# An mLSTM scan's element-wise steps: scalings and decay exponentials on ScalarE, the mask behind them, two directions joined from PSUM, and silu formed without GpSimd

## The chip, the cores and the metric

The kernel runs on one core of a Trainium2 chip. Its time is the device time of one execution in microseconds (us). Five engines work side by side, each through its own row of instructions, strictly in order: TensorE (PE, matrix products into PSUM banks), VectorE (DVE), ScalarE (ACT), GpSimd (POOL) and SyncE (SP, which issues most DMAs). A profile counts PE's loading of weights as a line of its own (PEld).

## The reference, cut to what matters

The program is one step of a two-layer network over 1024 sample tokens and 128 prompt tokens, 1024 features wide. The first layer has four bidirectional mLSTM heads and grouped-query attention side by side, the second has neighbourhood attention. Each branch is multiplied by silu(z) of the same input projection.

```python
def step(carry, xs):                      # one 128-token chunk of one mLSTM head, one direction
    C, n, m = carry
    b = jnp.cumsum(lf, axis=-1)
    Dm = jnp.where(causal, b[..., :, None] - b[..., None, :] + li[..., None, :], -jnp.inf)
    ...
    P = jnp.exp(Dm - m_t[..., None]) * jnp.einsum('bhld,bhsd->bhls', qj, kj)
    num = w_inter[..., None] * jnp.einsum('bhvk,bhlk->bhlv', C, qj) + jnp.einsum('bhls,bhsv->bhlv', P, vj)
    den = ...
    h = num / jnp.maximum(jnp.abs(den), jnp.exp(-m_t))[..., None]
    ...
    wk = jnp.exp(g - m_new[..., None])
    C_new = a_st[..., None, None] * C + jnp.einsum('bhs,bhsv,bhsk->bhvk', wk, vj, kj)
...
ha = rmsnorm(h_f + rev(h_b), g_hn) * jax.nn.sigmoid(oa)
...
y = jnp.concatenate([ha, from_heads(hb)], axis=-1) * jax.nn.silu(z)
```

## The kernel before

The 1152 tokens are nine chunks of 128, taken three at a time as groups of 384 columns (`CW`). The program goes through phases: the norms and modulations (`front`), the gates and the projections of heads 0 and 1, the mLSTM scan of heads 0 to 3, grouped-query attention, its output, neighbourhood attention in eight pairs of heads, and the last output. Most of PE's work are projections in 32-bit split into a high and a low part: three products per block (L371, L372, L373) into one of two PSUM banks called `pj`. `weights` makes the high part of a weight tile on ACT (L114) and the low one on POOL (L115, 128x1024).

The order of the work around the change is not written by hand. A scheduler builds each engine's row from the program and its own model of durations, so that an edit in one step can move its neighbours. Only in the attention phases does PE's row follow the program text. In the scan, the projections of the next heads, the second layer's modulation rows (L252, a custom DVE operation on 128x512) and the scan's own steps are mixed by it.

One head of the scan (`mlstm`) runs as follows.
- Seven times, `update` scales the keys of one chunk per direction into `kw` (L670, two buffers), multiplies them with the values into a bank called `o` (L673), and DVE adds the product to the decayed state `cs` (L680). Head by head this is a chain of eight.
- Then three groups. `decays` takes the tile `e`, which `decays_load` fetched by DMA (L644, issued in ACT's row while the head before was in the same group, three buffers), and turns it into decays: subtract (L653, POOL), mask (L656, POOL), exponential (L658, ACT). DVE multiplies by the scores (L711). Matmuls fill one PSUM bank per direction, `po` (L717 and L719, banks named `s`).
- `den` is formed from the banks; DVE scales both directions (L732) and adds them (L733) into `hs`. ACT squares `hs` (L736), POOL forms the reciprocal root (L133, L134), POOL scales `hs` (L739), and PE transposes it (L106, bank `tr`). DVE multiplies by the gate tile `gt` (L750).

The gate tile comes from projections: `oev` (tanh L609 on ACT, scaling L610 on POOL, by `ghn`) and `zev`, which calls `silu_gate` (tanh L395 on ACT, L396 on POOL, product L397 on DVE). `silu_gate` also serves the gates `gz` of both attentions: 48 calls, 12 of them in the mLSTM heads.

Of the kernel before, what the change touches and what calls it, by code (L numbers as in the profile page):

```python
# [12 lines left out]
AF = mybir.ActivationFunctionType  # L13
ALU = mybir.AluOpType
# [4 lines left out]
P = 128  # L19
# [9 lines left out]
NEG = -1e30  # L29
# [10 lines left out]
class Kern:  # L40
# [350 lines left out]
    def silu_gate(self, out, ps):  # L391

        nc = self.nc
        th = self.st([P, CW], n="th")
        nc.scalar.activation(th, ps, AF.Tanh, scale=0.5)  # L395
        nc.gpsimd.tensor_scalar(th, th, 0.5, 0.5, ALU.mult, ALU.add)  # L396
        nc.vector.tensor_tensor(out, th, ps, ALU.mult)  # L397


    def gates_proj(self, h):  # L400
# [165 lines left out]
    def mlstm_proj(self, hd):  # L566

        nc = self.nc
        new = lambda n: self.u(([P, NT, P + (n == "v")] if n in "kv" else [P, T]), n=n)
        o = {}  # L570

        def tok3(src, dst):
            for g in range(NC):
                pt = self.ps("ptr")
                for i in range(3):
                    s = (3 * g + i) * P
                    self.flipped(pt[:, i * P : (i + 1) * P], src[:, s : s + P])
                self.evac(dst[:, 3 * g : 3 * g + 3, 0:P], pt[:, :CW].rearrange("p (a b) -> p a b", b=P))

        def qev(c, ps):  # L580
            if c == 0:
                o["q"] = new("qT")
            for y, x in self.rows(o["q"], c, ps):
                self.evac(y, x)

        def kev(c, ps):
            if c == 0:
                o["kT"] = new("kT")
            for y, x in self.rows(o["kT"], c, ps):
                nc.scalar.activation(y, x, AF.Copy, scale=float(P) ** -0.5)  # L590
            if c == 2:
                o["k"] = new("k")
                tok3(o["kT"], o["k"])

        def vev(c, ps):
            if c == 0:
                o["vT"] = new("vT")
            for y, x in self.rows(o["vT"], c, ps):
                self.evac(y, x)
            if c == 2:  # L600
                v = o["v"] = new("v")
                nc.vector.memset(v[:, :, P], 1.0)
                tok3(o["vT"], v)

        def oev(c, ps):
            if c == 0:
                o["g"] = new("gate")
            g = o["g"][:, c * CW : (c + 1) * CW]
            nc.scalar.activation(g, ps, AF.Tanh, scale=0.5)  # L609
            nc.gpsimd.tensor_scalar(g, g, 1.0, self.ghn[:, hd : hd + 1], ALU.add, ALU.mult)  # L610

        def zev(c, ps):
            z = self.st([P, CW], n="z")
            self.silu_gate(z, ps)
            g = o["g"][:, c * CW : (c + 1) * CW]
            nc.vector.tensor_tensor(g, g, z, ALU.mult)

        return lambda: [o[n] for n in ("q", "kT", "k", "v", "g")], (qev, kev, vev, oev, zev)
# [28 lines left out]
    def decays(self, hd, g, t):  # L647

        nc = self.nc
        e, wb = t[:, 0:2], t[:, 2:4]  # L650
        ev = e.rearrange("p d (c l) -> p d c l", l=P)
        av = self.nat[:, 0, 3 * g : 3 * g + 3, :].rearrange("p c (d h) -> p h d c", d=2)[:, hd]
        nc.gpsimd.tensor_tensor(ev, av[:, :, :, None].to_broadcast([P, 2, 3, P]), ev, ALU.subtract)  # L653
        for d in range(2):
            s = 1 if d == 0 else -1
            nc.gpsimd.affine_select(out=ev[:, d], in_=ev[:, d], pattern=[[0, 3], [s, P]], compare_op=ALU.is_ge, fill=NEG, base=0, channel_multiplier=-s)  # L656
        ef = e.rearrange("p d l -> p (d l)")
        nc.scalar.activation(ef, ef, AF.Exp)  # L658
        return e, wb

    def mlstm(self, hd, cs, order, qT, kT, k, v, gt):
        nc, a = self.nc, self.a
        nat = self.nat
        P1 = P + 1

        def update(chs):

            kw = self.t("kw", 2, [P, 2, P])
            for d in range(2):
                nc.gpsimd.tensor_tensor(kw[:, d, :], k[:, chs[d], :], nat[:, 1, chs[d], 4 * d + hd : 4 * d + hd + 1].to_broadcast([P, P]), ALU.mult)  # L670
            pu = self.ps("o")
            for d in range(2):
                nc.tensor.matmul(pu[:, d * P1 : (d + 1) * P1], kw[:, d, :], v[:, chs[d], :], start=True, stop=True)  # L673
            return [pu[:, d * P1 : (d + 1) * P1] for d in range(2)]
# [28 lines left out]
        for g in range(NC):  # L703
            e, wb = self.decays(hd, g, ts[g])
            ql = qT[:, g * CW : (g + 1) * CW]
            nc.vector.tensor_tensor(wb, wb, ql[:, None, :].to_broadcast([P, 2, CW]), ALU.mult)
            pst = self.ps("s")
            for i in range(3):
                s = (3 * g + i) * P
                nc.tensor.matmul(pst[:, i * P : (i + 1) * P], kT[:, s : s + P], qT[:, s : s + P], start=True, stop=True)  # L710
            nc.vector.tensor_tensor(e, e, pst[:, None, :CW].to_broadcast([P, 2, CW]), ALU.mult)  # L711
            po = [self.ps("s") for _ in range(2)]
            for i in range(3):
                ch = 3 * g + i
                for d in range(2):
                    o = po[d][:, i * P1 : (i + 1) * P1]
                    nc.tensor.matmul(o, e[:, d, i * P : (i + 1) * P], v[:, ch, :], start=True, stop=ch == 8)  # L717
                    if ch < 8:
                        nc.tensor.matmul(o, wb[:, d, i * P : (i + 1) * P], cs[d][:, ch, :], start=False, stop=True)  # L719
            den = self.sm(6)  # L720
            hs = self.t("hs", 2, [P, 3, P])
            hb = self.t("hb", 1, [P, 3, P])
            for d in range(2):
                pv = po[d][:, : 3 * P1].rearrange("p (c l) -> p c l", l=P1)
                nc.scalar.activation(den[:, 3 * d : 3 * d + 3], pv[:, :, P], AF.Abs)
            floor = nat[:, 2, 3 * g : 3 * g + 3, :].rearrange("p c (d h) -> p d c h", d=2)[:, :, :, hd]
            dv = den[:, :6].rearrange("p (d c) -> p d c", d=2)
            nc.vector.tensor_tensor(dv, dv, floor, ALU.max)
            nc.vector.reciprocal(den[:, :6], den[:, :6])
            for d in range(2):  # L730
                pv = po[d][:, : 3 * P1].rearrange("p (c l) -> p c l", l=P1)
                nc.vector.tensor_tensor((hs, hb)[d], pv[:, :, 0:P], den[:, 3 * d : 3 * d + 3, None].to_broadcast([P, 3, P]), ALU.mult)  # L732
            nc.vector.tensor_tensor(hs, hs, hb, ALU.add)  # L733
            ss = self.sm(3)
            for i in range(3):
                nc.scalar.activation(hb[:, i, :], hs[:, i, :], AF.Square, accum_out=ss[:, i : i + 1])  # L736
            rs = self.sm(3)
            self.rstd(rs[:, :3], ss[:, :3], P)
            nc.gpsimd.tensor_tensor(hs, hs, rs[:, :3, None].to_broadcast([P, 3, P]), ALU.mult)  # L739
            if hd + 1 < HA:  # L740
                self.ts.append(self.decays_load(hd + 1, g))
            pt = self.ps("tr")
            for i in range(3):
                self.flipped(pt[:, i * P : (i + 1) * P], hs[:, i, :])
            for i in range(3):
                ch = 3 * g + i
                src = pt[:, i * P : (i + 1) * P]
                if ch < 8:
                    src = self.by_rows(src)
                nc.vector.tensor_tensor(self.cols(y, ch), src, self.cols(gt, ch), ALU.mult)  # L750
# [153 lines left out]
    def gqa_scores(self, Q, kv, new, prs):  # L904

        nc = self.nc
        zero = self.zero[:, 0:1].to_broadcast([P, CW])
        for hh in range(2):
# [11 lines left out]
            r = self.smg(1)  # L920
            nc.scalar.activation(pr, pr, AF.Exp, bias=nm, scale=-1.0, accum_out=r)
            nc.vector.reciprocal(r, r)
            for c in range(NC):
                nc.gpsimd.tensor_scalar(pr[:, c, :], pr[:, c, :], r, 1.0, ALU.mult, ALU.mult)  # L924
            prs.append(pr)
            yield

# [94 lines left out]
    def ctx_steps(self, S, V, tmp, po=None, banks=("tr", "s")):  # L1022
# [9 lines left out]
        r = self.sm(2)  # L1032
        for hh in range(2):
            nc.scalar.activation(pr[:, hh, :], s[hh], AF.Exp, bias=nm[:, hh : hh + 1], accum_out=r[:, hh : hh + 1])
        nc.vector.reciprocal(r[:, :2], r[:, :2])
        nc.gpsimd.tensor_tensor(pr, pr, r[:, :2, None].to_broadcast([P, 2, P]), ALU.mult)
        yield
# [212 lines left out]
    def na_unit(self, terms, v, vc, bias, j, po):  # L1250
# [15 lines left out]
        for hh in range(2):  # L1266
# [5 lines left out]
            r = self.sm(1)  # L1272
            nc.scalar.activation(x, x, AF.Exp, bias=nm, scale=-1.0, accum_out=r)  # L1273
            nc.vector.reciprocal(r, r)  # L1274
            nc.gpsimd.tensor_scalar(x, x, r, 1.0, ALU.mult, ALU.mult)  # L1275
            tr = self.ps(("tr", "ptr")[hh])
            for i in range(nk):
                self.flipped(tr[:, i * P : (i + 1) * P], x[:, i * P : (i + 1) * P])
# [14 lines left out]
    def run(self):  # L1293
# [11 lines left out]
        with self.phase("front"):  # L1305
# [2 lines left out]
            self.mod0 = self.const([P, KB, 2, 2], "mod0")  # L1308
            self.shift[0], self.scale[0] = self.mod0[:, :, 0], self.mod0[:, :, 1]
            self.ghn = self.const([P, 4], "ghn")  # L1310
            nc.vector.tensor_scalar(self.ghn, self.par[:, 80:84], 0.5, None, ALU.mult)
            h = [self.chunk("h") for _ in range(NC)]


# [323 lines left out]
```

## Time and profile before

| | |
|---|---|
| median of 3 runs | 1554.34 us (1553.78 to 1555.73) |
| the profiled execution | 1554.8 us, of which its span 1553.0 |
| granted TensorE clock, mean | 0.995 |
| busy in the span: PE, DVE, ACT, POOL | 1499.3, 846.4, 653.0, 609.9 us |
| chain of work that ended last | PE 83%, DVE 6%, DMA 3%, POOL 2%, ACT 2%, issue 2% |
| instructions | 27156 |

A line of the profile such as L653 is a line of the kernel file; a group is written output<-inputs with partitions x elements. Time under an engine is time in which it worked; the idle time before an instruction is put down to what released it last. An engine that is idle costs nothing unless the chain that ends last runs through it.

### The profile page before, as it was taken

The page shows a single profiled execution, that of the slowest core. Times are in us where ns is not written, and L with a number is a line of the kernel's source. Part 1 is how long each engine was busy: PE and PEld are TensorE (multiplying, and loading weights), DVE is VectorE, ACT ScalarE, POOL GpSimd, SP SyncE. Part 2 cuts the span into 40 slices and gives each one's busy share as a digit, 9 for nine tenths or more (in the row PEclk, how much of TensorE's full clock was granted, in tenths as well). Part 3 has the DMA queues.
Part 4 walks back from the last instruction along what each step waited for, and adds up shares of the span by engine and source line. Part 5 has one row for each costly group of instructions (what it writes and reads, how often), then busy time and mean ns, then how long its engine had stood idle before and what let it go on. Part 6 is the DMA issues. An engine that isn't in the chain of part 4 may idle for free.

```text
span 1553.0 us, 27156 instructions
## 1 busy us (share of the span) xinstructions
PE 1499.3 (97%) x10164; PEld 1380.9 (89%) x10164; DVE 846.4 (55%) x2342; ACT 653.0 (42%) x1573; POOL 609.9 (39%) x830
## 2 busy tenths in 40 slices
PE   7899999999999899999999999999999999999998
PEld 5799998999999888777788989999999999989886
DVE  5732997974547856665465452435243434345532
ACT  4622212112235767778344452445243434345411
POOL 3414645644445835577133332333142314243200
PEclk9999999999999999999999999999999999999999
DMA  9212634431220000021334212131213121225342
GB/s 354 81 42 102 219 124 182 158 113 65 104 93 32 17 23 32 24 72 49 134 108 159 74 52 87 34 105 27 90 44 97 31 84 39 87 76 151 128 130 82
DMA packets 75011, 143.80 MB, mean 93 GB/s; under 512 B 15928, under 2 KB 46848, under 8 KB 74880
## 3 DMA queue, kind: packets, MB, share of 16 engines
q1 hardware_dynamic: 70294, 126.91, 24.7%
q10 hardware_dynamic: 4586, 15.16, 2.6%
q8 instruction: 80, 1.31, 0.3%
q14 instruction: 51, 0.42, 0.1%
HBM read 115.47 MB, written 21.86 MB: 88 GB/s over the span
## 4 chain that ended last, share of the span: by engine, by line
PE 83%; DVE 6%; DMA 3%; POOL 2%; ACT 2%; issue 2%; SPq 0%; DVEq 0%; POOLq 0%; ACTq 0%
PE pj L371 12%; PE pj L373 12%; PE pj L372 12%; PE pj L386 7%; PE pj L387 7%; PE pj L388 7%; PE s L914 4%; PE ptr L106 4%; PE o L954 4%; PE o L1288 4%; PE s L1265 3%; PE tr L106 3%; DVE mj L252 2%; PE pj L106 2%; DMA wm<-in_w_mod_dram 1%
## 5 line engine op out<-in xcount | busy, mean ns | idle before, releaser
L371 PE MATMUL pj<-hh,whi 128*128 128x384 f32 x1168 | 399.9, 342 | 2.9 <-DVE z L397 2.5
L373 PE MATMUL pj<-hh,wlo 128*128 128x384 f32 x1168 | 396.9, 340 | 0.0
L372 PE MATMUL pj<-hl,whi 128*128 128x384 f32 x1168 | 396.0, 339 | 0.0
L371 PEld LDWEIGHTS pj<-hh,whi 128*128 128x128 f32 x1168 | 219.9, 188 | 6.1 <-DVE z L397 2.8
L372 PEld LDWEIGHTS pj<-hl,whi 128*128 128x128 f32 x1168 | 220.0, 188 | 1.3
L373 PEld LDWEIGHTS pj<-hh,wlo 128*128 128x128 f32 x1168 | 219.8, 188 | 1.2 <-issue 0.5
L115 POOL TENSOR_TENSOR wlo<-raw,whi 128x1024 fp32r<-128x1024 f32 (+1 forms) x75 | 156.4, 2096 | 154.6 <-ACT whi L114 105.8
L1275 POOL TENSOR_SCALAR sb<-sb,sm 128x512 f32<-128x512 f32 (+1 forms) x128 | 84.7, 667 | 242.6 <-DVE sm L1274 234.1
L924 POOL TENSOR_SCALAR pr<-pr,smg 128x384 f32<-128x384 f32 x192 | 109.2, 585 | 81.3 <-PE pj L106 41.9
L386 PE MATMUL pj<-whi,hh 128*128 128x256 f32 x432 | 122.5, 284 | 0.3 <-DVE nr L789 0.3
L387 PE MATMUL pj<-wlo,hh 128*128 128x256 f32 x432 | 122.5, 284 | 0.0
L388 PE MATMUL pj<-whi,hl 128*128 128x256 f32 x432 | 122.4, 283 | 0.0
L915 DVE CUSTOM_DVE_ANT_0 pr<-s,zero 128x384 f32<-128x384 f32 x192 | 103.6, 553 | 25.1 <-PE s L914 21.6
L386 PE MATMUL pj<-whi,yh 128*128 128x512 f32 x288 | 114.2, 397 | 2.1 <-DVE o L1083 1.5
L387 PE MATMUL pj<-wlo,yh 128*128 128x512 f32 x288 | 113.8, 395 | 0.0
L388 PE MATMUL pj<-whi,yl 128*128 128x512 f32 x288 | 113.4, 394 | 0.0
L252 DVE CUSTOM_DVE_ANT_0 mj<-wm,cb 128x512 f32<-128x512 f32 x128 | 110.8, 865 | 3.8 <-DMA wm<-in_w_modT_dram 1.8
L1273 ACT ACTIVATE sb<-sb,sm 128x512 f32<-128x512 f32 (+1 forms) x128 | 88.8, 695 | 51.6 <-DVE sm L1271 47.2
L914 PE MATMUL s<-Kst,Q 128*128 128x384 f32 x384 | 107.6, 372 | 0.7 <-DVE smg L915 0.7
L114 ACT CAST whi<-raw 128x1024 fp32r<-128x1024 f32 (+1 forms) x89 | 81.1, 930 | 22.9 <-DMA raw<-in_w_out_dram 6.6
L1271 DVE CUSTOM_DVE_ANT_1 sb<-s,bias 128x512 f32<-128x512 f32 (+1 forms) x112 | 72.9, 664 | 25.0 <-PE ptr L106 14.4
L386 PEld LDWEIGHTS pj<-whi,hh 128*128 128x128 f32 x432 | 81.3, 188 | 1.4 <-issue 0.5
(351 smaller groups left out, 2955.7 us busy)
## 6 DMA issues: line engine op xcount, KB each, us to landing
wm<-in_w_modT_dram SPq DMA_DIRECT2D x32, 512.0 KB, 5.9
raw<-in_w_c_dram SPq DMA_DIRECT2D x25, 512.0 KB, 3.6
raw<-in_w_ab_dram SPq DMA_DIRECT2D x20, 512.0 KB, 3.5
e<-rbd ACTq DMA_DIRECT2D x12, 768.0 KB, 5.5
bias<-in_na_bias_dram SPq DMA_DIRECT2D x16, 576.0 KB, 4.8
wm<-in_w_mod_dram SPq DMA_DIRECT2D x16, 512.0 KB, 7.0
raw<-in_w_out_dram SPq DMA_DIRECT2D x16, 512.0 KB, 3.6
y<-yd SPq DMA_DIRECT2D x18, 448.0 KB, 3.4
```

The source lines that it names most:

```text
L106: self.nc.tensor.transpose(out, in_, self.ident)
L115: (eng_lo or nc.gpsimd).tensor_tensor(lo, src, hi.bitcast(F32), ALU.subtract)
L252: nc.vector.tensor_tensor_reduce(junk, w[:, b, :], cb[:, r, :], 1.0, 0.0, ALU.mult, ALU.add, mp[:, hf, q // 4, 2 * (q % 4) + b, r : r + 1])
L371: nc.tensor.matmul(ps[:, :CW], a, hh, start=k == 0, stop=False)
L372: nc.tensor.matmul(ps[:, :CW], a, hl, start=False, stop=False)
L373: nc.tensor.matmul(ps[:, :CW], b, hh, start=False, stop=k == KB - 1)
L386: nc.tensor.matmul(ps[:, :width], hh, a, start=k == 0, stop=False)
L387: nc.tensor.matmul(ps[:, :width], hh, b, start=False, stop=False)
L388: nc.tensor.matmul(ps[:, :width], hl, a, start=False, stop=k == KB - 1)
L914: nc.tensor.matmul(s[:, :CW], x, y, start=part == 0, stop=part == 1)
L915: nc.vector.tensor_tensor_reduce(pr[:, c, :], s[:, :CW], zero, -1.0, -NEG, ALU.add, ALU.min, m3[:, c : c + 1])
L924: nc.gpsimd.tensor_scalar(pr[:, c, :], pr[:, c, :], r, 1.0, ALU.mult, ALU.mult)
```

## The change

- `silu_gate`: tanh(x/2)·x + x is formed in one fused DVE operation; POOL's step goes. This is twice silu(x), and the factor is taken out elsewhere: `ghn` is 0.25 instead of 0.5 times its parameter, the probabilities of both attentions are scaled by 0.5 in the POOL step that they already have (L924, L1275 before), and the context softmax of the second layer doubles its row sum in a new DVE step ahead of the reciprocal (12 of them).
- `oev`: the scaling of the gate moves from POOL to ACT.
- `decays`: subtraction and exponential become six ACT exponentials of 128x128 with a per-row bias and scale −1. The mask comes behind them on POOL, two per group as before, filling 0.
- `update`: the two `kw` scalings move from POOL to ACT (64 in all).
- `h`: per chunk, ACT scales the backward direction from PSUM into `hb`, and one DVE operation scales the forward one from PSUM and adds it. It was two products of three chunks and one sum.
- The scaling of `hs` moves from POOL to ACT, one per chunk.

```diff
 def silu_gate(self, out, ps):
     nc.scalar.activation(th, ps, AF.Tanh, scale=0.5)
-    nc.gpsimd.tensor_scalar(th, th, 0.5, 0.5, ALU.mult, ALU.add)
-    nc.vector.tensor_tensor(out, th, ps, ALU.mult)
+    nc.vector.scalar_tensor_tensor(out, th, 1.0, ps, ALU.add, ALU.mult)
 ...
 # oev
-    nc.gpsimd.tensor_scalar(g, g, 1.0, self.ghn[:, hd : hd + 1], ALU.add, ALU.mult)
+    nc.scalar.activation(g, g, AF.Identity, scale=self.ghn[:, hd : hd + 1], bias=self.ghn[:, hd : hd + 1])
 ...
 # decays
-    av = self.nat[:, 0, 3 * g : 3 * g + 3, :].rearrange("p c (d h) -> p h d c", d=2)[:, hd]
-    nc.gpsimd.tensor_tensor(ev, av[:, :, :, None].to_broadcast([P, 2, 3, P]), ev, ALU.subtract)
     for d in range(2):
         s = 1 if d == 0 else -1
-        nc.gpsimd.affine_select(out=ev[:, d], in_=ev[:, d], ..., fill=NEG, base=0, channel_multiplier=-s)
-    ef = e.rearrange("p d l -> p (d l)")
-    nc.scalar.activation(ef, ef, AF.Exp)
+        for i in range(3):
+            nc.scalar.activation(ev[:, d, i], ev[:, d, i], AF.Exp, bias=self.nat[:, 0, 3 * g + i, 4 * d + hd : 4 * d + hd + 1], scale=-1.0)
+        nc.gpsimd.affine_select(out=ev[:, d], in_=ev[:, d], ..., fill=0.0, base=0, channel_multiplier=-s)
 ...
 # update
-    nc.gpsimd.tensor_tensor(kw[:, d, :], k[:, chs[d], :], nat[:, 1, chs[d], 4 * d + hd : 4 * d + hd + 1].to_broadcast([P, P]), ALU.mult)
+    nc.scalar.activation(kw[:, d, :], k[:, chs[d], :], AF.Identity, scale=nat[:, 1, chs[d], 4 * d + hd : 4 * d + hd + 1])
 ...
 # mlstm, per group
-    for d in range(2):
-        pv = po[d][:, : 3 * P1].rearrange("p (c l) -> p c l", l=P1)
-        nc.vector.tensor_tensor((hs, hb)[d], pv[:, :, 0:P], den[:, 3 * d : 3 * d + 3, None].to_broadcast([P, 3, P]), ALU.mult)
-    nc.vector.tensor_tensor(hs, hs, hb, ALU.add)
+    for i in range(3):
+        f, b = (po[d][:, i * P1 : i * P1 + P] for d in range(2))
+        nc.scalar.activation(hb[:, i, :], b, AF.Identity, scale=den[:, 3 + i : 4 + i])
+        nc.vector.scalar_tensor_tensor(hs[:, i, :], f, den[:, i : i + 1], hb[:, i, :], ALU.mult, ALU.add)
 ...
-    nc.gpsimd.tensor_tensor(hs, hs, rs[:, :3, None].to_broadcast([P, 3, P]), ALU.mult)
+    for i in range(3):
+        nc.scalar.activation(hs[:, i, :], hs[:, i, :], AF.Identity, scale=rs[:, i : i + 1])
 ...
 # context softmax
+    nc.vector.tensor_scalar(r[:, :2], r[:, :2], 2.0, None, ALU.mult)
     nc.vector.reciprocal(r[:, :2], r[:, :2])
```

How this moves the rows, at the end of head 0's second group and the start of its third. The number behind a name counts tiles and differs between the kernels; `e_1665` before and `e_1677` after are the third group's decays. POOL's row before:

```order
L133 TENSOR_SCALAR sm_1661<-sm_1657 128x3
L653 TENSOR_TENSOR e_1665<-nat,e_1665 128x768
L134 TENSOR_TENSOR sm_1661<-sm_1661,mhalf 128x3
L396 TENSOR_SCALAR th_1940<-th_1940 128x384
L656 AFFINE_SELECT e_1665<-e_1665 128x384 x2
L739 TENSOR_TENSOR hs_1648<-hs_1648,sm_1661 128x384
```

POOL's row after, at the same place:

```order
L133 TENSOR_SCALAR sm_1671<-sm_1667 128x3
L134 TENSOR_TENSOR sm_1671<-sm_1671,mhalf 128x3
L655 AFFINE_SELECT e_1677<-e_1677 128x384 x2
L638 COPY cs_2035<-n0T 128x1
L115 TENSOR_TENSOR wlo_2046<-raw_2043,whi_2045 128x1024
```

Of POOL's six steps before, the subtraction, the silu step and the scaling of `hs` are gone; the reciprocal root and the masks are left.

ACT's row before, from the DMA that fetches the third group's `e` to the second tanh behind it (`hb_1649` and `hs_1648` belong to the second group):

```order
L644 DMA e_1665<-rbd 128x1536
L658 ACTIVATE e_1612<-e_1612 128x768
L609 ACTIVATE gate_1833<-pj_1875 128x384
L736 ACTIVATE hb_1649,sm_1657<-hs_1648 128x128 x3
L395 ACTIVATE th_1940<-pj_1914 128x384
L658 ACTIVATE e_1665<-e_1665 128x768
L395 ACTIVATE th_1977<-pj_1951 128x384
```

And after:

```order
L643 DMA e_1677<-rbd 128x1536
L608 ACTIVATE gate_1845<-pj_1887 128x384
L609 ACTIVATE gate_1845<-gate_1845,ghn 128x384
L729 ACTIVATE hb_1656<-s_1643,sm_1654 128x128 x3
L733 ACTIVATE hb_1656,sm_1667<-hs_1655 128x128 x2
L654 ACTIVATE e_1677<-e_1677,nat 128x128 x2
L733 ACTIVATE hb_1656,sm_1667<-hs_1655 128x128
L654 ACTIVATE e_1677<-e_1677,nat 128x128 x4
L395 ACTIVATE th_1952<-pj_1926 128x384
L737 ACTIVATE hs_1655<-hs_1655,sm_1671 128x128 x3
L395 ACTIVATE th_1988<-pj_1962 128x384
```

ACT now holds the next group's six exponentials between the squares of this one, and the tanh of the `z` gate and the scaling of `hs` stand behind them.

The end of head 1's chain of updates and the start of head 2's, in POOL's row before (`k_1399` are head 1's keys, `k_2236` head 2's, `wlo_2501` the low part of a weight tile):

```order
L670 TENSOR_TENSOR kw_2298<-k_1399,nat 128x128 x2
L670 TENSOR_TENSOR kw_2306<-k_1399,nat 128x128 x2
L115 TENSOR_TENSOR wlo_2501<-raw_2498,whi_2500 128x1024
L670 TENSOR_TENSOR kw_2314<-k_1399,nat 128x128 x2
L670 TENSOR_TENSOR kw_3077<-k_2236,nat 128x128 x2
```

The end of head 1's chain in ACT's row after (`k_1396` are its keys, `k_2245` head 2's, `whi_2524` the high part of a weight tile):

```order
L667 ACTIVATE kw_2299<-k_1396,nat 128x128 x2
L722 ACTIVATE sm_2371<-s_2357 128x3
L101 COPY k_2245<-ptr_2246 128x384
L114 CAST whi_2524<-raw_2522 128x1024
L667 ACTIVATE kw_2307<-k_1396,nat 128x128 x2
L667 ACTIVATE kw_2315<-k_1396,nat 128x128 x2
L101 COPY k_2245<-ptr_2256 128x384
L667 ACTIVATE kw_2323<-k_1396,nat 128x128 x2
```

The scalings no longer stand with POOL's weight splits, but between ACT's key copies and weight casts.

More of the change, by code (lines that the diff above doesn't have):

```diff
@@ L651, in decays @@
         ev = e.rearrange("p d (c l) -> p d c l", l=P)
-        av = self.nat[:, 0, 3 * g : 3 * g + 3, :].rearrange("p c (d h) -> p h d c", d=2)[:, hd]
-        nc.gpsimd.tensor_tensor(ev, av[:, :, :, None].to_broadcast([P, 2, 3, P]), ev, ALU.subtract)
         for d in range(2):
             s = 1 if d == 0 else -1
-            nc.gpsimd.affine_select(out=ev[:, d], in_=ev[:, d], pattern=[[0, 3], [s, P]], compare_op=ALU.is_ge, fill=NEG, base=0, channel_multiplier=-s)
-        ef = e.rearrange("p d l -> p (d l)")
-        nc.scalar.activation(ef, ef, AF.Exp)
+            for i in range(3):
+                nc.scalar.activation(ev[:, d, i], ev[:, d, i], AF.Exp, bias=self.nat[:, 0, 3 * g + i, 4 * d + hd : 4 * d + hd + 1], scale=-1.0)
+            nc.gpsimd.affine_select(out=ev[:, d], in_=ev[:, d], pattern=[[0, 3], [s, P]], compare_op=ALU.is_ge, fill=0.0, base=0, channel_multiplier=-s)
         return e, wb
@@ L923, in gqa_scores @@
             for c in range(NC):
-                nc.gpsimd.tensor_scalar(pr[:, c, :], pr[:, c, :], r, 1.0, ALU.mult, ALU.mult)
+                nc.gpsimd.tensor_scalar(pr[:, c, :], pr[:, c, :], r, 0.5, ALU.mult, ALU.mult)
             prs.append(pr)
@@ L1274, in na_unit @@
             nc.vector.reciprocal(r, r)
-            nc.gpsimd.tensor_scalar(x, x, r, 1.0, ALU.mult, ALU.mult)
+            nc.gpsimd.tensor_scalar(x, x, r, 0.5, ALU.mult, ALU.mult)
             tr = self.ps(("tr", "ptr")[hh])
@@ L1310, in run @@
             self.ghn = self.const([P, 4], "ghn")
-            nc.vector.tensor_scalar(self.ghn, self.par[:, 80:84], 0.5, None, ALU.mult)
+            nc.vector.tensor_scalar(self.ghn, self.par[:, 80:84], 0.25, None, ALU.mult)
             h = [self.chunk("h") for _ in range(NC)]
```

## The prediction

> **What bounds the kernel now.** I read the page's busy line first, then the span cut at its phases, then the waits of TensorE (PE), then the places of the longest waits.
>
> ```profile
> PE 1499.3 (97%) x10164; PEld 1380.9 (89%) x10164; DVE 846.4 (55%) x2342; ACT 653.0 (42%) x1573; POOL 609.9 (39%) x830
> ```
>
> PE is the bound: 1499.3 of 1553.0 us. The change adds and removes no matmul, so it can only win back idle time of PE, 53.7 us in all, or time lost to a lowered clock, or add to both. Next, the span by phase. Columns: stretch, length, busy us of PE, PE's weight loads, DVE, ACT and POOL (instructions in brackets), granted clock of PE, DMA share, GB/s.
>
> ```profile
> 140.00:340.00 200.00, 185.68 (x1167) 180.51 (x1166) 169.00 (x412) 41.51 (x111) 105.69 (x122) 0.99 0.43 153
> 340.00:500.00 160.00, 159.38 (x1135) 158.37 (x1134) 88.74 (x233) 55.61 (x235) 76.30 (x126) 1.00 0.22 79
> 560.00:740.00 180.00, 173.91 (x1360) 143.73 (x1358) 114.65 (x471) 135.77 (x243) 109.71 (x169) 1.00 0.14 47
> 900.00:1400.00 500.00, 495.79 (x3713) 474.80 (x3712) 209.72 (x600) 209.97 (x487) 158.57 (x174) 1.00 0.22 67
> ```
>
> The mLSTM scan of heads 0 to 2 fills 140 to 340, and head 3 lies past it. In 140:340 PE idles 200 − 185.7 = 14.3 us, and the busiest helper is DVE (169 of 200); ACT is nearly empty (41.5). In 340:500 PE idles 0.6 us: nothing to win there. Grouped-query attention (560:740) idles 6.1, neighbourhood attention (900:1400) 4.2. So all that the change can win in the scan is among the 14.3, and its waits are these (what PE waited for: us in total, times, longest), with the one of the attention phase behind them:
>
> ```profile
> PE pj L371 <- DVE z L397: 2.5, 2, 1.9
> PE o L673 <- POOL kw L670: 2.4, 2, 1.2
> PE tr L106 <- POOL hs L739: 2.1, 2, 1.3
> PE s L717 <- DVE hs L732: 1.7, 1, 1.7
> PE ptr L106 <- ACT k L101: 1.5, 4, 0.6
> PE s L717 <- DVE e L711: 0.6, 1, 0.6
> ...
> PE tr L106 <- POOL pt L1036: 6.1, 4, 2.2
> ```
>
> Five of the seven lines name an operation that the change replaces or moves: z, kw, hs twice, e. Their sum is 2.5 + 2.4 + 2.1 + 1.7 + 0.6 = 9.3 us, 0.6% of the time: the ceiling of waits to win.
>
> **The change part by part.** Durations of the operations (busy us, mean ns | idle time ahead of them, and what ended it):
>
> ```profile
> L653 POOL TENSOR_TENSOR e<-nat,e 128x768 f32<-128x768 f32 x12 | 24.2, 2016 | 16.0 <-DMA e<-rbd 12.2 <-PE pj L373 3.6
> L396 POOL TENSOR_SCALAR th<-th 128x384 f32<-128x384 f32 x48 | 27.7, 576 | 70.8 <-ACT th L395 69.4 <-issue 1.3
> L670 POOL TENSOR_TENSOR kw<-k,nat 128x128 f32<-128x128 f32 x64 | 30.5, 498 | 75.7 <-PE o L673 75.7
> L739 POOL TENSOR_TENSOR hs<-hs,sm 128x384 f32<-128x384 f32 x12 | 11.2, 930 | 0.6
> L610 POOL TENSOR_SCALAR gate<-gate,ghn 128x384 f32<-128x384 f32 x12 | 9.4, 782 | 15.4 <-ACT gate L609 15.1
> L658 ACT ACTIVATE e<-e 128x768 f32<-128x768 f32 x12 | 10.1, 845 | 39.5 <-POOL e L656 39.5
> L736 ACT ACTIVATE hb<-hs 128x128 f32<-128x128 f32 x36 | 10.7, 300 | 19.7 <-DVE hs L733 19.7
> L1034 ACT ACTIVATE pt<-s,sm 128x128 f32<-128x128 f32 x24 | 8.6, 362 | 15.0 <-PE o L1288 13.4 <-ACT sb L1273 0.8 <-DVE sm L1031 0.8
> L345 ACT ACTIVATE x<-ptr,mod,mod 128x128 f32<-128x128 f32 x18 | 8.3, 458 | 0.0
> L732 DVE TENSOR_TENSOR hb<-s,sm 128x384 f32<-128x384 f32 x12 | 6.6, 546 | 0.0
> L733 DVE TENSOR_TENSOR hs<-hs,hb 128x384 f32<-128x384 f32 x12 | 8.9, 744 | 0.2
> L680 DVE SCALAR_TENSOR_TENSOR cs<-cs,astb,o 128x129 f32<-128x129 f32 x56 | 17.0, 343 | 16.0 <-PE o L673 16.0
> ```
>
> POOL loses L653, L396, L670, L739 and L610: 24.2 + 27.7 + 30.5 + 11.2 + 9.4 = 103.0 us, to some 507. ACT gains 72 exponentials, 64 kw, 36 hb and 36 hs scalings of 128x128, and 12 gate scalings, and loses L658. A 128x128 activation cost 300 ns without a scale from a tile (L736), 362 with one such operand (L1034), 458 with two (L345). Nearly all the new ones have one, so 208 × 0.362 = 75.3; the gates, three times as wide and with two operands, I estimate at 0.64 each, from L658's 845 at twice their width, 7.7 in all. ACT: 75.3 + 7.7 − 10.1 = +73, to 726 (between 208 × 0.300 and 208 × 0.458, +60 to +93). DVE gives up two products and a sum per group (about 0.55 + 0.55 + 0.74 = 1.84, twelve times 22.1) for three fused operations like L680's (36 × 0.343 = 12.3), and gets twelve tiny ones in the context softmax (1.9 by the 0.16 us reciprocal shown below): −8, to 838. None of these sums is a gain by itself; the waits decide. Term by term, then.
>
> *1. The gate z.* Its longest wait, 1.9 us, stands here (start us, duration, engine, line, tile; in brackets the engine's idle time):
>
> ```profile
> 197.03 0.47 ACT L395 ACTIVATE th<-pj 128x384 f32<-128x384 f32 x1
> 197.51 2.08 POOL L653 TENSOR_TENSOR e<-nat,e 128x768 f32<-128x768 f32 x1
> 199.56 1.29 POOL L134 TENSOR_TENSOR sm<-sm,mhalf 128x3 f32<-128x3 f32 x1
> 200.84 0.51 POOL L396 TENSOR_SCALAR th<-th 128x384 f32<-128x384 f32 x1
> 201.38 0.55 DVE L397 TENSOR_TENSOR z<-th,pj 128x384 f32<-128x384 f32 x1 [0.49 <-POOL th L396]
> ```
>
> ACT had the tanh ready at 197.50, but POOL's share of the silu stood behind L653 and L134 to 200.84; the `pj` bank came free at 201.93. Both L653 and L396 go. DVE then takes z right behind its own work, some 3 us earlier, in PE's cover. I take 2.0 of the 2.5. The wait also cost clock; granted clock is the third column from the right:
>
> ```profile
> 202.00:204.00 2.00, 2.00 (x6) 2.00 (x7) 2.00 (x4) 1.66 (x3) 2.00 (x4) 0.52 0.00 0
> 204.00:206.00 2.00, 2.00 (x10) 1.90 (x10) 2.00 (x8) 0.49 (x1) 2.00 (x3) 0.63 0.00 0
> ```
>
> After 1.9 us of idling, PE ran at 0.52 and 0.63 for two windows of 2 us: (1 − 0.52) × 2 + (1 − 0.63) × 2 = 1.7 us lost. Without the wait it comes back. Term: −3.7 (0 if another DVE job stands there, −4.2 if both waits go).
> [...]
>
> *2. hs behind POOL.* L739's 930 ns become three ACT scalings, 3 × 0.362 = 1.09: no shorter. But what is ahead on POOL (L653 of the next group) goes, and in the new order the three transposes that wait for hs stand 58 instructions of PE further back. Against that, the reciprocal root ahead of hs stays on POOL, and ACT may have a tanh ahead. Of 2.1 I take −1.0 (0 to −2.1).
>
> *3. po's banks and e.* Two products released the `s` banks in 1.1 us; now three ACT copies and one last fused step take 3 × 0.362 + 0.343 = 1.4, one engine feeding the other. That is 0.3 longer, but the sum L733 is gone, and DVE, which is what stood in the way, has 0.8 less per group. L658 and L711 wait for POOL less. Of 1.7 + 0.6 I take −0.8 (+1.0 to −2.3).
>
> *4. kw.* Here one of its two waits, 1.2 us:
>
> ```profile
> 239.19 2.42 POOL L115 TENSOR_TENSOR wlo<-raw,whi 128x1024 fp32r<-128x1024 f32 x1 [0.24 <-ACT whi L114]
> 239.28 2.88 DVE L252 CUSTOM_DVE_ANT_0 mj<-wm,cb 128x512 f32<-128x512 f32 x1
> 242.09 0.60 DVE L680 SCALAR_TENSOR_TENSOR cs<-cs,astb,o 128x129 f32<-128x129 f32 x2
> 242.84 0.35 PE L673 MATMUL o<-v,kw 128*128 128x129 f32 x1 [1.24 <-POOL kw L670]
> ...
> L252 DVE CUSTOM_DVE_ANT_0 mj<-wm,cb x128: 675/691/2877, 157.0 to 340.4; 128x512 f32<-128x512 f32 x128
> ```
>
> POOL's weight split L115 delays kw, but DVE has L252 beside it, 2.88 us where the median (second of the three numbers, ns) is 691, and L680, which empties the `o` bank, ends at 242.69. So with kw early on ACT the matmul still waits for `o` until about 242.7. What was a wait for kw becomes one for L680. Term: −0.3 (0 to −2.4).
>
> *5. New standing on ACT.* ACT issues in order, and now holds, in the scan, the next head's six exponentials, some of them ahead of the last square and the hs scalings of the group before, and tanh behind. If e's DMA is late, ACT stands, and with it k copies, gate and z. L653's line has 12.2 us of such idle time on POOL, none of which shows among PE's waits. Six exponentials are 6 × 0.362 = 2.2 us against 0.85 before, 1.3 longer per group, and the kw scalings are 64 × 0.362 = 23 us more in ACT's row. What this costs PE no row shows; the nearest is its wait for ACT's k copies, 1.5 us. With ACT's work in the scan about doubled I let that double: +1.5 (0, since ACT is idle for 158 of 200 us, to +7, somewhat over half of rival A's 11.8).
>
> *6. Context softmax.* A doubling on DVE is put ahead of the reciprocal:
>
> ```profile
> 579.34 1.71 POOL L924 TENSOR_SCALAR pr<-pr,smg 128x384 f32<-128x384 f32 x3 [4.64 <-DVE smg L922]
> 579.62 0.16 DVE L1035 RECIPROCAL sm<-sm 128x2 f32<-128x2 f32 x1
> 581.01 0.61 POOL L1036 TENSOR_TENSOR pt<-pt,sm 128x256 f32<-128x256 f32 x1
> ```
>
> L1036, for which PE waited 6.1 us, starts at 581.01, 1.2 after the reciprocal's end: POOL's three L924 hide 0.16 more. Term 0; without that cover 4 × 0.16 = +0.6. The 36 silu gates outside the scan lose their POOL step too, in phases where PE idles 0.6 to 6.1 us for other things: 0.
>
> Sum: −3.7 − 1.0 − 0.8 − 0.3 + 1.5 = −4.3. The profiled execution took 1554.8 (1.8 of it outside the span): 1550.5. It lies 0.46 over the median of the three runs, 1554.34, so **1550.0**.
>
> **The rivals.**
> *A, slower: ACT stands at e's transfer.* It takes, in us, least, median and most:
>
> ```profile
> DMA to landing us min/median/max: 3.9/5.5/8.3
> ```
>
> At the first group of each of three heads the exponentials could stand 8.3 − 5.5 = 2.8 us with the k copies and gates behind them: 8.4, and two clock drops, 3.4. With the gains of terms 1 to 4 (−5.8): 11.8 − 5.8 = +6.0, 1560. It decides once ACT's stands cost PE more than 5.8 + 3.1 = 8.9 us. Against it: e is loaded a head ahead, into three buffers, and ACT is busy 41.5 of 200 us. 12%.
> *B, same: the next wait takes the place.* DVE stays at 160 or more of 200 us and L252 beside L115 stays long; the waits for kw, z and hs change names. Then −1 to −2: 1552.5 to 1554. For it, term 4's place; against it, that term 1's wait has no DVE work behind it but 0.55. 28%.
> *C, larger gain:* POOL free of 103 us lets L115 run elsewhere than beside L252 and all waits of 9.3 us go with the clock's 1.7: −11, 1543 to 1546. 15%.
> *Forecast,* 1547 to 1551: 45%.
>
> **How the numbers follow.** 0.2% of 1554 is 3.1 us, about what a measurement tells from no change; faster means under 1551.2, slower over 1557.5. Forecast and C are faster: 0.60. B is the same: 0.28. A is slower: 0.12. The range for 8 in 10 leaves out half of C and most of A: 1545 to 1557; the forecast's own is 1547 to 1551.
>
> **What would show it.** Right: POOL near 507 busy, ACT 726, DVE 838; PE idle in 140:340 near 10; z no longer behind POOL, clock 1.00 where it was 0.52; waits of PE for L680 and ACT k still there. Wrong: PE's `pj` waiting for a tanh or gate behind exponentials, or transposes waiting for hs on ACT (A); or L252's longest still 2.9 and PE idle at 13 or more (B).

## The result, and the profile after

The changed kernel took 1547.05 us (median of 6 runs, 1544.08 to 1549.56) beside 1555.66 for the kernel before (6 runs, 1553.78 to 1561.55); the ratio is 0.9935 (95% interval 0.992 to 0.9949), about 10 us faster; the two medians lie 8.6 us apart. The two profiled executions differ by 6.9 us of span (1553.0 and 1546.1). Of the remaining 2 to 3 us the traces show nothing: the profiled execution of before was one of its short ones (1554.8; its median beside the experiments was 1557.0 to 1558.2).

The busy line of the page after, and the scan's window 140 to 340 (columns as in the prediction):

```profile
PE 1499.5 (97%) x10164; PEld 1380.5 (89%) x10164; DVE 827.6 (54%) x2354; ACT 713.9 (46%) x1781; POOL 512.1 (33%) x682
```

```profile
140.00:340.00 200.00, 192.47 (x1215) 186.90 (x1214) 158.18 (x420) 81.18 (x249) 57.80 (x53) 1.00 0.44 156
```

PE's idle time in the scan fell from 14.3 to 200 − 192.5 = 7.5 us; that is the span's gain. ACT doubled there (41.5 to 81.2), POOL fell from 105.7 to 57.8. The waits of PE in the same window (us in total, times, longest):

```profile
PE pj L371 <- DVE z L396: 2.4, 2, 1.6
PE tr L106 <- ACT hs L737: 1.8, 3, 0.9
PE ptr L106 <- ACT k L101: 1.3, 3, 0.6
PE s L716 <- DVE cs L677: 1.1, 1, 1.1
PE ptr L106 <- DVE vT L103: 0.3, 1, 0.3
PE o L670 <- DVE cs L677: 0.2, 1, 0.2
PE s L716 <- DVE cs L637: 0.2, 1, 0.2
```

The waits for kw (2.4), for hs and e ahead of the `s` banks (1.7 + 0.6) are gone. The waits for z are as long in sum as before, 2.4, but stand elsewhere. At 202, where PE had idled 1.9 us and run at a granted clock of 0.52 and 0.63 after it, there is nothing now, and the clock stays at 1.00 (it is third from the right; the 0.75 us of idling in the second row end at 205.45, with the shorter of the two waits for z):

```profile
202.00:204.00 2.00, 2.00 (x13) 2.00 (x12) 2.00 (x1) 0.01 (x1) 2.00 (x1) 1.00 0.00 0
204.00:206.00 2.00, 1.25 (x9) 0.96 (x7) 2.00 (x6) 0.00 (x0) 0.09 (x1) 1.00 0.34 49
```

The longest wait of the changed kernel's scan is this one (timeline: start, duration, engine, line; rows of other instructions left out):

```profile
283.47 2.93 POOL L115 TENSOR_TENSOR wlo<-raw,whi 128x1024 fp32r<-128x1024 f32 x1 [1.50 <-ACT whi L114]
...
284.45 2.49 DVE L252 CUSTOM_DVE_ANT_0 mj<-wm,cb 128x512 f32<-128x512 f32 x1
...
286.88 0.54 DVE L396 SCALAR_TENSOR_TENSOR z<-th,pj 128x384 f32<-128x384 f32 x1
287.48 0.44 PE L371 MATMUL pj<-hh,whi 128*128 128x384 f32 x1 [1.63 <-DVE z L396]
```

z no longer waits for POOL's silu step. It stands behind DVE's L252, which lasts until just after POOL's weight split L115 beside it: L115 ends at 286.40, L252 at 286.94. The wait for `cs` at 239.96 has the same cause: L252 of 2.81 us beside L115 of 2.42.

### The profile page after: what moved, and what is told of

It reads as the page before. It is cut to its first block, busy times and chain, and to the rows that moved or that the text cites. A ratio compares the mean times of both kernels' runs of the same rounds, so it can differ in the third digit from the quotient of the medians.

```text
span 1546.1 us, 27173 instructions
## 1 busy us (share of the span) xinstructions
PE 1499.5 (97%) x10164; PEld 1380.5 (89%) x10164; DVE 827.6 (54%) x2354; ACT 713.9 (46%) x1781; POOL 512.1 (33%) x682
## 4 chain that ended last, share of the span: by engine, by line
PE 49%; DVE 1%; DMA 1%; ACT 1%; POOL 1%; issue 0%; DVEq 0%; POOLq 0%; ACTq 0%
PE pj L371 7%; PE pj L372 7%; PE pj L373 7%; PE pj L387 6%; PE pj L386 6%; PE pj L388 6%; PE o L1287 4%; PE s L1264 3%; PE ptr L106 2%; PE tr L106 2%; DMA y<-yd 1%; POOL wlo L115 0%; ACT yh L114 0%; DVE yl L115 0%; DVE sb L1270 0%
## 5 line engine op out<-in xcount | busy, mean ns | idle before, releaser
L115 POOL TENSOR_TENSOR wlo<-raw,whi 128x1024 fp32r<-128x1024 f32 (+1 forms) x75 | 157.4, 2108 | 296.7 <-ACT whi L114 265.8
L252 DVE CUSTOM_DVE_ANT_0 mj<-wm,cb 128x512 f32<-128x512 f32 x128 | 107.3, 838 | 5.3 <-DMA wm<-in_w_modT_dram 3.2
```

The costliest lines, as they stand in the source:

```text
L115: (eng_lo or nc.gpsimd).tensor_tensor(lo, src, hi.bitcast(F32), ALU.subtract)
L252: nc.vector.tensor_tensor_reduce(junk, w[:, b, :], cb[:, r, :], 1.0, 0.0, ALU.mult, ALU.add, mp[:, hf, q // 4, 2 * (q % 4) + b, r : r + 1])
```

## The experiments

Twelve kernels ran, each in five rounds beside the kernel before. "Idle" is PE's idle time in 140:340 of each profile, as above (before: 14.3); it is read from one execution, and with kw taken back it stands 3.6 us over the changed kernel's at the same ratio. It leaves out what a lowered clock costs: summed over stretches of 4 us, worked out as in the prediction's first term, the scan lost an estimated 5.1 us to it with join and hs alone, 3.4 with kw alone, 1.7 in the kernel before, with all but silu, with all but kw and in the kernel before with the low weights on DVE, and nothing in the others (with decays, silu and the low weights on DVE read from the whole window alone, at 1.00).

| kernel | ratio to before | 95% interval | idle, us |
|---|---|---|---|
| changed kernel | 0.9935 | 0.992 to 0.9949 | 7.5 |
| silu alone | 1.0 | 0.9987 to 1.0014 | 15.0 |
| join and hs alone | 1.0007 | 0.9995 to 1.002 | 12.6 |
| kw alone | 1.0015 | 1.0002 to 1.0028 | 15.2 |
| decays alone | 0.9986 | 0.9971 to 1.0001 | 12.1 |
| all but decays | 0.9986 | 0.9973 to 1.0 | 14.4 |
| all but silu | 0.9967 | 0.9954 to 0.998 | 12.7 |
| all but kw | 0.994 | 0.9923 to 0.9956 | 11.1 |
| all but join and hs | 0.9932 | 0.9911 to 0.9953 | 7.0 |
| decays and silu | 0.9947 | 0.9933 to 0.9962 | 10.2 |
| changed, low weights on DVE | 0.9896 | 0.9881 to 0.9911 | 2.9 |
| before, low weights on DVE | 0.9974 | 0.9963 to 0.9985 | 10.1 |
| decays, silu, low weights on DVE | 0.9895 | 0.9877 to 0.9913 | 3.2 |

### One part alone

The edits are the hunks of the change: of the silu, `silu_gate`, `ghn`, the factors 0.5 and the doubling; of the join and hs, the last two of `mlstm`; of kw, the one of `update`; of the decays, the one of `decays`. Silu alone:

> The kernel before with the fused silu alone (silu_gate, ghn 0.25, the 0.5 in the probabilities, the doubling in the context softmax). Theory T (each wait goes with the part that names its operation): the wait of 1.9 us for z at 202 shrinks, since POOL's L653 stands ahead of L134 but no longer ahead of z; idle time of PE in 140:340 falls from 14.3 to about 12.3, the 1.7 us of lowered clock at 202 to 206 go, the time falls by 3 to 4 us. Theory R (DVE is what stands in the way: behind POOL's weight split L115 its L252 takes 2.5 to 2.9 us and z stands behind that): z waits as long elsewhere, the idle time stays at 13 to 14.3, the time falls by 0 to 2 us.

Join and hs alone:

> The kernel before with the joining of the two directions and the scaling of hs changed alone. T: the waits of PE for hs (2.1 behind POOL, 1.7 behind DVE) lose 1.8 of 3.8 us, time -1 to -3 us; L653 and L396 still stand on POOL and z's wait with its lowered clock stays. R: DVE's busy time in the scan falls by about 10 us for all heads and with it the waits behind DVE wherever they stand: PE idle in 140:340 falls by 3 us or more, time -3 to -5 us.

Kw alone:

> The kernel before with the kw scalings on ACT alone. T: the two waits for kw of 1.2 us become waits for L680 behind L252; time -0.3 us, within 0 to -1. Rival K (kw itself was late, and the chain behind it moves with it): the 2.4 us of kw and the 1.4 us of waiting for L680 go, idle in 140:340 about 10.5, time -3 to -4 us.

Decays alone:

> The kernel before with the decays alone (six exponentials on ACT, mask behind). T: L653's 2.08 us go from POOL's row ahead of the silu step; the wait for z at 202 falls from 1.9 to under 0.5, its lowered clock goes, time -2 to -4 us, and the wait for e (0.6) stays or goes. R: no wait of PE goes for good, another takes z's place: time 0 to -2 us. If ACT's exponentials stand at e's transfer, PE waits for e or for ACT's k copies and the time is +1 to +6 us.

Measured: 1557.55, 1557.49, 1559.84 and 1553.87 us beside 1557.01. By the ratios only the decays come near what T gave them (some 2 us of 2 to 4, with an interval that reaches no change). Silu gave nothing, nor did join and hs, the kw part cost time, and the sum of the four is no gain. R doesn't hold for join and hs either: DVE worked 160.1 us in 140:340 instead of 169.0, and the time stayed. The waits that the parts name shrink or pass to another engine, and others take their place. With silu alone, around 202:

```profile
199.04 2.09 POOL L652 TENSOR_TENSOR e<-nat,e 128x768 f32<-128x768 f32 x1
201.09 1.30 POOL L134 TENSOR_TENSOR sm<-sm,mhalf 128x3 f32<-128x3 f32 x1
...
202.35 1.58 POOL L655 TENSOR_SCALAR_AFFINE_SELECT e<-e 128x384 f32<-128x384 f32 x2
203.90 1.25 POOL L738 TENSOR_TENSOR hs<-hs,sm 128x384 f32<-128x384 f32 x1
...
205.21 0.55 PE L106 MATMUL tr<-cc,hs 128*128 128x128 f32 x3 [1.50 <-POOL hs L738]
```

The wait for z is down to 0.81 us, but the decays' subtraction (here L652) still heads POOL's row, and PE now waits 1.50 us for `hs`, three lines later in the same row. With the decays alone it is the other way round:

```profile
197.58 1.25 POOL L737 TENSOR_TENSOR hs<-hs,sm 128x384 f32<-128x384 f32 x1
...
198.79 0.97 POOL L656 TENSOR_SCALAR_AFFINE_SELECT e<-e 128x384 f32<-128x384 f32 x1
...
199.74 0.51 POOL L396 TENSOR_SCALAR th<-th 128x384 f32<-128x384 f32 x1
...
200.28 0.55 DVE L397 TENSOR_TENSOR z<-th,pj 128x384 f32<-128x384 f32 x1 [0.89 <-POOL th L396]
...
200.89 0.44 PE L371 MATMUL pj<-hh,whi 128*128 128x384 f32 x1 [1.01 <-DVE z L397]
```

`hs` is early, and the silu step behind the mask holds z. In the kw run PE's wait for kw became one for `cs`, 4.2 us in all, against 2.4 + 1.4 before: the exchange that the prediction's fourth term described, and the rival K is out.

### One part taken back

The changed kernel, with one hunk as before. Without the decays:

> The changed kernel with the decays as before (subtraction and mask on POOL, one exponential on ACT), all else changed. Against the kernel before. Theory I (the scan's idle time of PE is one store that several engines fill in turn; each part alone only hands its wait to the next, so the gain of about 10 us needs them together and each part taken back costs 2 to 5 us): -5 to -8 us, PE idle in 140:340 between 9 and 12. Rival S (one part carries it, by the runs of one part the decays, -2 us alone): -0 to -3 us here and close to -10 us when any other part is taken back.

Without the silu:

> The changed kernel with silu's second step back on POOL and its factors as before. I: -5 to -8 us, z waits behind POOL again, though not behind L653. S: -9 to -11 us.

Without kw:

> The changed kernel with the kw scalings back on POOL. I: -5 to -8 us; PE waits for kw on POOL behind the weight split L115 again, about 2.4 us. S: -9 to -11 us. By the prediction's fourth term (0.3 us) the time would be 0.3 us over the changed kernel's.

Without the join and the scaling of hs:

> The changed kernel with the joining of the two directions on DVE and the scaling of hs on POOL as before. I: -5 to -8 us; DVE's busy time in 140:340 is back at 165 or more, and PE waits for hs behind DVE (about 1.7 us) and POOL. S: -9 to -11 us. By the prediction's second and third terms: 1.8 us over the changed kernel's.

Measured: 1556.31, 1553.24, 1549.66 and 1546.44 us beside 1557.57. Neither theory holds as written. I is wrong for kw and for the join, which cost nothing when taken back; S is wrong for the silu, which costs half the gain. Without the decays 1.3 us of the gain are left, without the silu 4.3. Without the decays POOL stood 5.8 us at `e`'s transfer ahead of the subtraction, and the weight split behind both gave PE its longest wait, 2.43 us. Without the silu 2.4 of the 12.7 us of idling stand elsewhere than at silu's step: ACT stood at `e`'s transfer, with the scaling that frees an `s` bank behind it in its row.

```profile
269.87 0.69 ACT L655 ACTIVATE e<-e,nat 128x128 f32<-128x128 f32 x2 [2.78 <-DMA e<-rbd]
...
271.38 0.49 PE L715 MATMUL s<-v,e 128*128 128x129 f32 x2 [2.43 <-ACT hb L730]
```

So the price of taking silu back isn't all POOL's row; this profile is also the longest of the kernel's twelve executions. The same stand costs PE 2.7 us with kw taken back. With kw back on POOL its old wait is back,

```profile
PE o L670 <- POOL kw L667: 2.4, 2, 1.2
```

and still the ratio is 0.994 against 0.9935.

### Decays and silu

Both hunks, nothing else:

> The kernel before with two parts alone: the decays and the fused silu. Theory P (these two carry the gain, and only together: L653 and L396 stood in one row on POOL between PE's bank and DVE, and taking one leaves the other step to wait; kw, the join, hs and the gate's scaling change nothing measurable): -8 to -11 us against before, PE idle in 140:340 between 7 and 9. Rival Q (one of the others is needed too, since each part alone gave 0 to -2 us): -3 to -5 us, idle 11 or more.

Measured 1549.67 beside 1558.15, ratio 0.9947: P's time, with 10.2 us of idling rather than 7 to 9. The two together give 0.53%, and alone 0 and 0.14%; the interval of the two together overlaps the changed kernel's. At the place of the two fences above, POOL, DVE and ACT are now on time, and PE waits for neither z nor hs:

```profile
196.37 0.47 ACT L395 ACTIVATE th<-pj 128x384 f32<-128x384 f32 x1
...
196.96 0.55 DVE L396 SCALAR_TENSOR_TENSOR z<-th,pj 128x384 f32<-128x384 f32 x1
197.40 0.82 POOL L736 TENSOR_TENSOR hs<-hs,sm 128x384 f32<-128x384 f32 x1
```

Among what is left of its waits are z (1.6) and `cs` (1.5 and 1.1), behind a long L252, ACT's k copies (1.5) and kw on POOL (1.2).

### The low weight parts on DVE

```diff
-                w = self.weights(a["w_ab"][5 * hd + b], new=new)
+                w = self.weights(a["w_ab"][5 * hd + b], "lo" if new is None else "", new=new)
```

This takes 15 of the weight splits L115 from POOL to DVE. On the changed kernel:

> The changed kernel with the low weight parts of 15 blocks (heads 1 to 3, and what is loaded of them ahead of the scan) made on DVE instead of POOL. Theory D (what is left of the waits in the scan is DVE standing in L252 for 2.5 to 2.8 us instead of 0.69 whenever POOL's L115 runs beside it): L252's longest falls under 1.2 us, DVE's sum hardly changes (15 times 1.28 us in place of some 9 times 2.1), the waits for z and cs of 3.5 us halve, -1 to -3 us against the changed kernel. Rival E (DVE is the busiest helper, and its row makes the weights late): PE waits for wlo on DVE, +1 to +5 us.

On the kernel before:

> The kernel before with the same 15 low weight parts on DVE, nothing else. If the stretching of L252 beside L115 is by itself what the scan loses, the time falls by 3 us or more; if POOL's row (L653, L396 ahead of z) is, by 0 to 2 us, since POOL is then free of 36 us but keeps those steps. By E: +1 to +5 us.

Measured: 1542.9 and 1553.86 us beside 1558.15. D holds, and its gain was larger than expected: 0.9896, a further 0.4% (some 6 us) under the changed kernel. PE's idle time in the scan fell by 7.5 − 2.9 = 4.6 us; the span of the profiled execution, the longest of five, fell by only 2.1, at a granted clock of 0.993 instead of 0.996. L252's times (ns, least, median, most) in the changed kernel, then with the weights on DVE:

```profile
L252 DVE CUSTOM_DVE_ANT_0 mj<-wm,cb x128: 647/691/2806, 158.9 to 335.2; 128x512 f32<-128x512 f32 x128
```

```profile
L252 DVE CUSTOM_DVE_ANT_0 mj<-wm,cb x128: 648/691/1006, 160.3 to 329.5; 128x512 f32<-128x512 f32 x128
```

And the scan's window and PE's waits in it, with the weights on DVE:

```profile
140.00:340.00 200.00, 197.06 (x1261) 193.29 (x1260) 156.19 (x439) 87.15 (x269) 29.25 (x45) 1.00 0.45 160
```

```profile
PE s L714 <- DVE e L708: 1.1, 2, 0.8
PE ptr L106 <- ACT k L101: 0.6, 1, 0.6
PE s L716 <- DVE cs L637: 0.5, 1, 0.5
PE ptr L106 <- ACT kT L589: 0.3, 1, 0.3
```

The waits for z and `cs` that stood behind L252 are gone. So is the one for hs on ACT (1.8), of which 0.93 at 262.89 and 0.60 at 273.59 had POOL's root L134 ahead of them and not L252; the edit also takes the splits out of POOL's row, and no run parts the two effects. DVE is no busier, 156.2 against 158.2 us, though it has the splits: on DVE a split takes 1.28 us (14 of the later phases are made there in the changed kernel too), where on POOL it held up L252 by 1.2 to 2.1, nine times. On the kernel before the same edit gives 0.9974, some 4 us, as expected if the stretched L252 is by itself a loss. That is more than the decays alone by the ratios, with intervals that overlap. PE still waits 2.4 us for hs on POOL and 2.8 for z there.

In the changed kernel's rows all nine stretched L252 end 0.54 to 0.55 us after the L115 beside them, less than the 0.69 (median) that L252 takes by itself, and with the splits on DVE it takes at most 1.0 us. Why DVE's operation lasts until POOL's is done, no run shows. L115 isn't the only one that does this. In the kernel before with the low weights on DVE, L252's longest is 1.97 us, beside the decays' subtraction, and it too ends 0.54 us after it:

```profile
184.49 1.52 POOL L653 TENSOR_TENSOR e<-nat,e 128x768 f32<-128x768 f32 x1
...
184.58 1.97 DVE L252 CUSTOM_DVE_ANT_0 mj<-wm,cb 128x512 f32<-128x512 f32 x1
```

### Which parts matter once that is gone

Decays, silu and the low weights on DVE:

> The kernel before with three parts: the decays, the fused silu, and the 15 low weight parts on DVE. If kw, the join, the scaling of hs and of the gate do nothing once decays and silu are done and L115 no longer holds DVE and POOL, the time is that of the changed kernel with the weights on DVE: -14 to -18 us against before, PE idle in 140:340 at 3 to 5 us. If those parts matter once the stretched L252 is gone (hs and kw on POOL, two products and a sum on DVE next in line), -9 to -13 us and idle of 6 us or more, with waits for hs on POOL or behind DVE's sum.

Measured 1540.05 beside 1557.27, ratio 0.9895, the same as with all of the change. Idle 3.2 us, and no wait of over 0.1 us for kw or hs: what POOL and DVE still do of them is hidden. It is, with the changed kernel with the low weights on DVE, the fastest of the study, 1.05% (0.9877 to 0.9913) under the kernel before.

```profile
140.00:340.00 200.00, 196.76 (x1261) 194.03 (x1260) 163.90 (x440) 53.16 (x161) 61.25 (x104) 1.00 0.45 160
```

## Why the prediction was right, point by point

The sign, the place (PE's idle time in 140:340) and the range were right; 1547.05 lies 3 us under the forecast of 1550.0, at the edge of its own range. That it lies inside is in part luck: the forecast started from 1554.34, and the kernel before took 1555.66 beside the change; 0.9935 of 1554.34 would be 1544.2. The gain in medians was 8.6 us where 4.3 was forecast. The missing 4 us are not in one term.

- *Term 1, z (−3.7).* The place was read rightly: the 1.9 us at 202 and the 1.7 us of clock behind them went. But it was said that z would stand in nothing but its own 0.55 us, and the sum of z's waits is 2.4 us as before, behind L252. So the term is −0.1 − 1.7 = −1.8. Over the whole span PE's busy time is the same (1499.3 and 1499.5), so that the 1.7 can't be seen in the sum.
- *Terms 2 and 3, hs and the banks (−1.8).* They measured −0.3 and −2.3. Their cause was wrong: the wait of 1.7 us at the `s` banks is also gone where the join and hs are as before, and taking that part back costs nothing. It stays with silu alone and with kw alone, and goes with the decays alone. In the kernel before, the DVE product that frees the bank stands behind L252, which the subtraction on POOL stretches to 1.55 us:

```profile
263.78 1.92 POOL L653 TENSOR_TENSOR e<-nat,e 128x768 f32<-128x768 f32 x1
...
264.69 1.55 DVE L252 CUSTOM_DVE_ANT_0 mj<-wm,cb 128x512 f32<-128x512 f32 x1
...
266.18 0.55 DVE L732 TENSOR_TENSOR hs<-s,sm 128x384 f32<-128x384 f32 x1
...
266.87 0.46 PE L717 MATMUL s<-v,e 128*128 128x129 f32 x2 [1.68 <-DVE hs L732]
```

- *Term 4, kw (−0.3).* The waits of PE for kw and for `o` fell from 3.8 to 0.2, with 1.1 more behind `cs` elsewhere: −2.5. Yet as the worth of kw's own edit −0.3 agrees with the runs within their noise: 0.994 without it against 0.9935 (intervals overlapping). The reason given, L252 behind L115, is the one that the run with the weights on DVE showed.
- *Term 5, standing on ACT (+1.5).* Mis-sized, and with the sign of a loss on the part that gained most. PE's wait for ACT's k copies went from 1.5 to 1.3.
- *Term 6 (0).* PE waited 6.2 us for the context softmax (6.1 before).

The step that failed is the sum itself: it gave every edit the wait that bore its name. By the runs the gain belongs to two edits, decays and silu, that shared POOL's row with the others. One of them, the subtraction, held PE through DVE's L252 as well; how much of its price went which way, no run tells.

Rival A didn't come in the changed kernel: ACT did stand at `e`'s transfer, but only 3.8 us in all, and none of PE's waits was behind it. Its mechanism was real: with the silu or kw taken back, such a stand cost PE 2.4 and 2.7 us. Of ACT's new steps kw stood longer, 36.0 us until PE's L670 was done, but PE had no wait for kw.

```profile
L654 ACT ACTIVATE e<-e,nat 128x128 f32<-128x128 f32 x72 | 22.6, 391 | 3.9 <-DMA e<-rbd 3.8
L667 ACT ACTIVATE kw<-k,nat 128x128 f32<-128x128 f32 x64 | 22.1, 394 | 43.1 <-PE o L670 36.0 <-issue 7.1
```

Rival B named the next wait, DVE in L252, and half of it came true: that is what was left, 3.5 of 7.3 us. Rival C's size (−11) was nearer to the measured gain than the forecast's 4.3, but not by its way: L115 still runs beside L252. Of the busy sums POOL came out as worked out (512 for 507), DVE 10 lower than said, and ACT 12 lower (714 for 726): equal activations run into each other, so that 72 of 391 ns are busy for 22.6 us, 314 each.

## What to carry to other kernels

Where one in-order engine serves several waits, a wait belongs to the whole row ahead of it and not to the instruction that is named (in the kernel before POOL's silu step started at 200.84 behind L653 and L134, on a tanh that was ready at 197.50): taking one step out hands the wait to the next, and two small edits that are worth little or nothing alone can be worth half a per cent together (ratios of 1.0 and 0.9986 alone, 0.9947 together). A step can also hold an engine that it gives nothing to, as POOL's subtraction and weight splits held an unrelated DVE operation here, for up to 2.88 us instead of 0.69 in the kernel before. Before the steps are spread over other engines, look for an instruction whose longest time is several times its median, and for what runs beside it: here one argument that moved 15 weight splits gave 0.4% on top of the whole change.

## What the runs showed of the hardware that was not expected

In these runs a longer idle time of PE was not always followed by a lowered clock. The 1.9 us at 202 in the kernel before were (0.52 and 0.63). Without the decays PE idled 2.43 us in one stretch and the clock stayed at 1.00, from 282 to 284 too:

```profile
280.45 0.44 PE L373 MATMUL pj<-hh,wlo 128*128 128x384 f32 x1 [2.43 <-POOL wlo L115]
```

```profile
280.00:282.00 2.00, 1.55 (x9) 1.55 (x10) 1.93 (x5) 0.00 (x0) 1.85 (x3) 1.00 0.42 35
```

Without the silu four waits of 0.43 to 0.57 us, one behind the other, were followed by a lowered clock:

```profile
150.26 0.55 PE L106 MATMUL ptr<-cc,kT 128*128 128x128 f32 x3 [0.57 <-ACT k L101]
151.46 0.55 PE L106 MATMUL ptr<-cc,kT 128*128 128x128 f32 x3 [0.43 <-DVE k L103]
152.57 0.44 PE L106 MATMUL ptr<-cc,c 128*128 128x128 f32 x2 [0.57 <-ACT k L101]
153.48 0.46 PE L717 MATMUL s<-cs,e 128*128 128x129 f32 x2 [0.48 <-DVE cs L638]
```

```profile
154.00:156.00 2.00, 2.00 (x11) 2.00 (x10) 0.06 (x1) 0.00 (x0) 1.95 (x1) 0.50 0.04 8
156.00:158.00 2.00, 2.00 (x11) 2.00 (x11) 0.61 (x2) 0.87 (x3) 0.00 (x0) 0.66 0.40 82
```

The loss is again 1 + 0.7 = 1.7 us. The kernel before has the same four waits in the same order (0.57, 0.43, 0.57 and 0.48 us, at 145.54 to 148.77), and there the clock stayed at 1.00:

```profile
148.00:150.00 2.00, 1.52 (x13) 1.32 (x13) 1.01 (x4) 0.75 (x1) 1.17 (x1) 1.00 0.00 0
150.00:152.00 2.00, 2.00 (x17) 1.94 (x16) 0.81 (x3) 0.17 (x1) 2.00 (x4) 1.00 0.04 8
152.00:154.00 2.00, 2.00 (x13) 2.00 (x12) 0.41 (x2) 0.00 (x0) 0.67 (x2) 1.00 0.77 217
```

So the 1.7 us of term 1 are a price that one execution paid for its waits and another didn't. What decides it, these rows don't show: the longest of the four waits is 0.57 us, with PE at work between them, and the 2.43 us above cost nothing.
